# Hymba-style decoder step: weight sums and up-times-gate products of the FFN from GpSimd to VectorE, two scratch stores from SyncE's queue to ScalarE's

## Chip, cores and metric

The kernel runs on one core of one Trainium2 chip. The metric is device time in microseconds (us) for one execution. Three executions of the kernel before took 1408.3, 1409.23 and 1413.17 us; the median is 1409.23 us.

The engines are TensorE (PE in the rows, with its weight loads as PEld), VectorE (DVE), ScalarE (ACT), GpSimd (POOL) and SyncE (SP), which only starts transfers. Each takes its instructions in a fixed order: what stands behind an instruction that waits, waits too.

## What is computed

One step of a decoder trunk for 1024 prompt positions and 8 sample rows (1032 columns in all): a token mixer (gMLP and Mamba-2 heads side by side), cross-attention into 256 memory tokens, a SwiGLU FFN with hidden size 2816, and a final RMSNorm. The change touches the FFN alone:

```python
def swiglu(hn, w_gate, w_up, w_down):
    return (jax.nn.silu(hn @ w_gate) * (hn @ w_up)) @ w_down
```

## The kernel before

All activations lie with features on the 128 partitions and columns in the free dimension. Every fp32 matmul is made of three fp32r matmuls: each operand is split into a high part (a cast on ScalarE) and a low part (a subtraction on VectorE), by `split_from` (lines 276 to 278); `mm3` (line 158) issues high-high, high-low and low-high.

In the FFN, gate and up are computed by a Strassen-Winograd scheme with seven products P1 to P7 in place of eight. The weights come in pairs of panels: `items` lists, for each pair number `fp` from 1 to 10, a gate item and then an up item, each with both column halves (q = 0 of 256 columns, q = 1 of 264). After fp 6 stand two short items, gate and up of fp 0 for q = 1 only (its q = 0 half is done ahead of the stage by `first_pair`). `gate_up(n)` runs through the seven products of item n in the order P1, P6, P2, P7, P5, P4, P3. A product of a full item is 24 matmuls, 12 for each half.

Three accumulator banks (X, Y, Z) per half are shared by the products: P6 and P7 and P4 follow each other in Y, P5 and P3 in Z, P1 and P2 in X. Between two products in one bank, VectorE has to read it (lines 1296, 1303, 1305; `t` and `u`/`g` in the rows): P7 waits for line 1296, P4 for line 1303, P3 for line 1305, each for its own half. ScalarE copies P1 out (line 1294).

`prepare(step)` makes the weight operand `fw` of one product, up to five products ahead (`AHEAD`, line 1262). At P6 it also forms four sums of the raw panels `fr` (lines 1248 to 1251, tiles `ws`): on VectorE for the first two items, on GpSimd for the other 20. There is room for one raw pair, so the next pair's panels (line 1231, from SyncE's queue) are loaded when the last reader of the panel they replace is done.

When an up item has its P4 and P3, its results `u` are multiplied by the gate's `g` on GpSimd (lines 1315 and 1321). Then `down_operands` (line 1349) forms on VectorE the differences that the down projection needs (line 1359, `dx`), and stores `u` and `dx` into the scratch `x_d` (line 1366). `down_sums` (line 1386) forms sums `ds` of the down weights `dr` (line 1391, loaded by line 1384) and stores them into `s_d` (line 1397). The tiles `dr`, `ds` and `dx` share four buffers (tag `qu`): a `ds` has to wait until the `dx` that lay in its buffer has been stored. All these loads and stores are issued by SyncE, in one order.

Program order is not the order on the engines: the program is written once, and a scheduler orders each engine's instructions by its own estimate of times (`schedule_with_timeline_sim=True`), with the evacuations of the banks preferred (`tc.high_priority()`). A change of engine therefore moves neighbouring instructions too.

Of the kernel before, what the change touches and what calls it, by code (L numbers as in the profile page):

```python
# [43 lines left out]
def hymba_step(ctx: ExitStack, tc: tile.TileContext, I, O):  # L44
# [1105 lines left out]
    with ExitStack() as c3:  # L1150
# [86 lines left out]
        def prepare(step):  # L1237

            n, o = divmod(step, 7)
            if n >= len(items):  # L1240
                return
            load_pair(n)
            (a11, a12), (a21, a22) = ((t[:, 0:512], t[:, 512:D]) for t in wraw[n])
            nm = order_of(n)[o]
            if nm == "P6":
                eng = nc.vector if n < 2 else nc.gpsimd
                s1, s2, s3, s4 = wsum[n] = [n3.tile([P, 512], F32, tag="ws", bufs=4, name=f"ws{n}_{i}") for i in range(4)]
                eng.tensor_tensor(s1, a21, a22, op=ALU.add)  # L1248
                eng.tensor_tensor(s2, s1, a11, op=ALU.subtract)  # L1249
                eng.tensor_tensor(s4, a12, s2, op=ALU.subtract)  # L1250
                eng.tensor_tensor(s3, a11, a21, op=ALU.subtract)
            src = {"P1": a11, "P2": a12, "P4": a22}[nm] if nm in ("P1", "P2", "P4") else wsum[n][("P5", "P6", "P7", "P3").index(nm)]
            t = wp.tile([P, D], F32R, tag=("whi", "wlo")[step % 2], name=f"fw{step}")
            split_from(t[:, 0:512], t[:, 512:D], src)
            wop[step] = tuple(t[:, s].rearrange("p (k n) -> p k n", n=P) for s in (slice(0, 512), slice(512, D)))
            if o == 6:
                load_pair(n + 1)
# [8 lines left out]
        def gate_up(n, between):  # L1266
            x, fp, qs = items[n]
            bank = {q: {} for q in qs}
            tmp = {q: temps(q) for q in qs}
            res = {}  # L1270
            for q in qs:
                res[q] = piece(f"{x}{fp}_{q}")[:, :, : WQ[q]].rearrange("p (j h) n -> p j h n", j=2)
            for o, nm in enumerate(order_of(n)):
                for s in range(7 * n + o, 7 * n + o + AHEAD + 1):
                    if s not in wop:
                        prepare(s)
                if o == 4:
                    form_differences()
                between(o)
                hi, lo = wop[7 * n + o]  # L1280
                for q in qs:
                    w = WQ[q]
                    p1, u2, u3 = tmp[q]
                    b = "XXYYZZ"[("P1", "P2", "P6", "P7", "P5", "P3").index(nm)] if nm != "P4" else "Y"
                    if b not in bank[q]:
                        bank[q][b] = (gbank if (n % 2 if len(qs) == 1 else q) == 0 else mbank)(f"{x}{b}{fp}_{q}")
                    fresh = nm in ("P1", "P6", "P5")
                    ps = bank[q][b][:, :w]
                    xh, xl = XQ[q][nm]
                    mm3(ps, lambda k: (hi[:, k, :], lo[:, k, :]), lambda k: (xh[:, k, :], xl[:, k, :]), range(4), fresh=fresh, done=nm in ("P2", "P4", "P3"))  # L1290
                    r = res[q]
                    with tc.high_priority():
                        if nm == "P1":
                            nc.scalar.copy(p1, ps)
                        elif nm == "P6":
                            nc.vector.tensor_add(u2, p1, ps)
                        elif nm == "P2":
                            if x == "g":
                                nc.scalar.activation(r[:, 0, 0, :], ps, AF.Silu)
                            else:  # L1300
                                nc.vector.tensor_mul(r[:, 0, 0, :], gates[q][:, 0, 0, :], ps)
                        elif nm == "P7":
                            nc.vector.tensor_add(u3, p1, ps)  # L1303
                        elif nm == "P5":
                            nc.vector.tensor_add(r[:, 1, 1, :], u3, ps)
                        elif nm == "P4":
                            nc.vector.tensor_add(r[:, 1, 0, :], p1, ps)
                        else:
                            nc.vector.tensor_add(r[:, 0, 1, :], u2, ps)
                    if nm == "P4":  # L1310
                        t = r[:, 1, :, :]
                        if x == "g":
                            nc.scalar.activation(t, t, AF.Silu)
                        else:
                            nc.gpsimd.tensor_tensor(t, t, gates[q][:, 1, :, :], op=ALU.mult)  # L1315
                    elif nm == "P3":
                        t = r[:, 0, 1, :]
                        if x == "g":
                            nc.scalar.activation(t, t, AF.Silu)
                        else:  # L1320
                            nc.gpsimd.tensor_tensor(t, t, gates[q][:, 0, 1, :], op=ALU.mult)
            for q in qs:
                if x == "g":
                    gates[q] = res[q]
                else:
                    differences.append(lambda q=q, r=res[q]: down_operands(fp, q, r))
# [27 lines left out]
        def down_operands(fp, q, r):  # L1354

            w = WQ[q]
            r = r.rearrange("p j h n -> p (j h) n")
            t = piece(f"dx{fp}_{q}", "qu")[:, 0:3, :w]
            sub = lambda o, x, y: nc.vector.tensor_tensor(o, x, y, op=ALU.subtract)
            sub(t[:, 1], r[:, 3], r[:, 1])  # L1360
            sub(r[:, 1], r[:, 1], r[:, 0])
            sub(t[:, 0], r[:, 3], r[:, 1])
            sub(t[:, 2], r[:, 2], t[:, 0])
            for i, src in ((0, r), (4, t)):
                m = src.shape[1]
                nc.sync.dma_start(x_d[i : i + m, fp, :, 256 * q : 256 * q + w].rearrange("o p n -> p o n"), src)

        def form_differences():
            for work in differences:
# [16 lines left out]
        def down_sums(fp):  # L1386

            (a11, a12), (a21, a22) = ((t[:, 0], t[:, 1]) for t in dn[fp])
            t = [n3.tile([P, 2, 512], F32, tag="qu", bufs=4, name=f"ds{fp}_{i}") for i in range(2)]
            s1, s2, s3, s4 = t[0][:, 0], t[0][:, 1], t[1][:, 0], t[1][:, 1]  # L1390
            op = lambda o, x, y, k: nc.vector.tensor_tensor(o, x, y, op=k)  # L1391
            op(s1, a21, a22, ALU.add)
            op(s2, s1, a11, ALU.subtract)
            op(s3, a11, a21, ALU.subtract)
            op(s4, a12, s2, ALU.subtract)
            for i in range(2):
                nc.sync.dma_start(s_d[2 * i : 2 * i + 2, :, fp, :].rearrange("s p n -> p s n"), t[i])

        def prepare_down(n):

# [274 lines left out]
```

## Time and profile before

| | |
|---|---|
| median of three executions | 1409.23 us |
| the profiled execution | 1412.27 us, its span 1410.4 us |
| TensorE busy | 1369.1 us, 97% of the span |
| VectorE busy | 957.9 us, 68% |
| ScalarE busy | 626.1 us, 44% |
| GpSimd busy | 304.1 us, 22% |
| TensorE clock granted | 0.99 of full speed in the mean |
| transfers | 232.66 MB, 165 GB/s in the mean |

Busy shares are means over stages with different limits. In a timeline, the first number is the start in us from the span's start, the second the duration; what stands in square brackets is the time that the engine was idle just before, and what it waited for. TensorE's matmuls are pipelined, so a duration overlaps the next start; distances between starts are the safe measure.

### The profile page before, as it was taken

What the parts mean: (1) busy time and instruction counts of PE and PEld (TensorE: products, weight loads), DVE (VectorE), ACT (ScalarE), POOL (GpSimd) and SP (SyncE); (2) the same over time, 40 slices, a digit from 0 to 9 for tenths busy, and PEclk for the clock granted to TensorE, in tenths of its full rate; (3) what the DMA queues carried; (4) which work ended last, traced back from release to release, by engine and by line L of the source; (5) the groups of instructions that cost most, each with busy time, mean ns of one, the idle gap of its engine ahead of it and who ended that gap; (6) DMA issues with size and microseconds to landing.
All of it is one profiled execution on the core that took longest, in us unless ns stands there. A gap on an engine that the chain in (4) does not pass through costs nothing. (4 is left out here: it accounts for less than half of the span.)

```text
span 1410.4 us, 26083 instructions
## 1 busy us (share of the span) xinstructions
PE 1369.1 (97%) x10315; PEld 1305.8 (93%) x10315; DVE 957.9 (68%) x2021; ACT 626.1 (44%) x1131; POOL 304.1 (22%) x263
## 2 busy tenths in 40 slices
PE   8999999999999999999999999999899999999997
PEld 8889988899999978988999999999899999999997
DVE  7886689734533877778988666657766675656685
ACT  5666545234332645844563333223332343543654
POOL 3321122201221300000002333433444321003020
PEclk9999999999999999999999999999999999999999
DMA  8531344310642578378424545443645569656664
GB/s 302 192 98 48 96 125 115 92 54 30 236 154 76 167 268 324 94 270 299 129 83 158 161 159 160 143 141 108 206 149 181 161 210 325 204 169 183 205 190 133
DMA packets 145530, 232.66 MB, mean 165 GB/s; under 512 B 8328, under 2 KB 91880, under 8 KB 145024
## 3 DMA queue, kind: packets, MB, share of 16 engines
q1 hardware_dynamic: 145264, 230.94, 50.6%
q8 instruction: 81, 1.33, 0.4%
q14 instruction: 41, 0.34, 0.1%
q10 hardware_dynamic: 144, 0.05, 0.0%
HBM read 179.16 MB, written 51.81 MB: 164 GB/s over the span
## 5 line engine op out<-in xcount | busy, mean ns | idle before, releaser
L149 DVE TENSOR_TENSOR wl<-wr,wh 128x1024 fp32r<-128x1024 f32 x87 | 109.1, 1256 | 34.6 <-ACT wh L148 34.3
L148 ACT CAST wh<-wr 128x1024 fp32r<-128x1024 f32 (+1 forms) x89 | 92.2, 1038 | 85.3 <-PE g_gv L172 25.1
L277 ACT CAST fw<-ws 128x512 fp32r<-128x512 f32 x88 | 54.4, 622 | 125.9 <-POOL ws L1249 54.8
L278 DVE TENSOR_TENSOR fw<-ws,fw 128x512 fp32r<-128x512 f32 x88 | 81.1, 923 | 38.3 <-ACT fw L277 38.2
L1248 POOL TENSOR_TENSOR ws<-fr 128x512 f32<-128x512 f32 x20 | 26.8, 1339 | 236.9 <-DMA fr<-in_w_gate_dram 169.5
L277 ACT CAST fw<-fr 128x512 fp32r<-128x512 f32 x66 | 40.8, 619 | 80.3 <-PE m_uZ L172 20.1
L1578 PE MATMUL m_d<-xP,dwhi 128*128 128x264 f32 x448 | 64.1, 285 | 0.0
L278 DVE TENSOR_TENSOR xP<-xsP,xP 128x512 fp32r<-128x512 f32 (+2 forms) x84 | 54.9, 694 | 12.8 <-ACT xP L277 12.3
L278 DVE TENSOR_TENSOR dwlo<-dw,dwhi 128x1024 fp32r<-128x1024 f32 x32 | 39.8, 1245 | 34.7 <-ACT dwhi L277 34.6
L1578 PE MATMUL g_d<-xP,dwhi 128*128 128x256 f32 x448 | 63.0, 283 | 0.0
L278 DVE TENSOR_TENSOR fw<-fr,fw 128x512 fp32r<-128x512 f32 x66 | 55.9, 848 | 8.1 <-ACT fw L277 7.7
L1578 PEld LDWEIGHTS m_d<-xP,dwhi 128*128 128x128 f32 x448 | 58.5, 189 | 0.0
L1578 PEld LDWEIGHTS g_d<-xP,dwhi 128*128 128x128 f32 x448 | 57.7, 191 | 0.0
L277 ACT CAST xP<-xsP 128x512 fp32r<-128x512 f32 (+2 forms) x84 | 45.3, 588 | 23.9 <-DMA xsP<-x_d 15.0
L172 PE MATMUL m_uY<-sP,fw 128*128 128x264 f32 x396 | 53.7, 284 | 1.4 <-DVE fw L278 1.4
L277 ACT CAST dwhi<-dw 128x1024 fp32r<-128x1024 f32 x32 | 33.6, 1050 | 47.7 <-PE m_d L1578 37.2
L172 PE MATMUL g_gY<-sP,fw 128*128 128x256 f32 (+1 forms) x396 | 53.1, 283 | 0.0
L172 PE MATMUL m_gY<-sP,fw 128*128 128x264 f32 x360 | 49.5, 286 | 3.5 <-DVE t L1303 3.5
L172 PEld LDWEIGHTS m_uY<-sP,fw 128*128 128x128 f32 x396 | 50.1, 189 | 1.7 <-DVE fw L278 1.7
L172 PEld LDWEIGHTS m_gY<-sP,fw 128*128 128x128 f32 x360 | 45.6, 188 | 5.0 <-DVE t L1303 4.7
L172 PEld LDWEIGHTS g_gY<-sP,fw 128*128 128x128 f32 x396 | 49.7, 190 | 0.3
L172 PE MATMUL g_uY<-sP,fw 128*128 128x256 f32 x360 | 48.3, 283 | 1.7 <-DVE t L1303 1.0
(556 smaller groups left out, 3842.6 us busy)
## 6 DMA issues: line engine op xcount, KB each, us to landing
xsP<-x_d SPq DMA_DIRECT2D x35, 520.0 KB, 5.9
wr<-in_w_q_dram SPq DMA_DIRECT2D x24, 512.0 KB, 3.9
fr<-in_w_gate_dram SPq DMA_DIRECT2D x22, 512.0 KB, 3.6
fr<-in_w_up_dram SPq DMA_DIRECT2D x22, 512.0 KB, 3.7
dr<-in_w_down_dram SPq DMA_DIRECT2D x22, 512.0 KB, 5.4
s_d<-ds SPq DMA_DIRECT2D x22, 512.0 KB, 3.5
wr<-in_w_in_dram SPq DMA_DIRECT2D x20, 512.0 KB, 3.6
dw<-s_d SPq DMA_DIRECT2D x20, 512.0 KB, 4.5
```

Source lines behind the costliest of these rows:

```text
L148: nc.scalar.copy(hi[:, s], r[:, s])
L149: (nc.gpsimd if i == 0 else nc.vector).tensor_tensor(lo[:, s], r[:, s], f(hi[:, s]), op=ALU.subtract)
L172: ins = nc.tensor.matmul(ps, lhs(k)[a], rhs(k)[b], start=(fresh and i == 0), stop=(i == n - 1), skip_group_check=not (fresh and done))
L277: nc.scalar.copy(dst_hi, src)
L278: (eng or nc.vector).tensor_tensor(dst_lo, src, f(dst_hi), op=ALU.subtract)
L1248: eng.tensor_tensor(s1, a21, a22, op=ALU.add)
L1578: nc.tensor.matmul(ps[:, : WQ[q]], wdn[n](k)[a], x_at(nm, q, k)[b], start=(i == 0), stop=(i == 3 * NPAIR - 1))
```

## The change

Three edits in the FFN: the four weight sums of every item are made on VectorE; the products of up with gate are made on VectorE; the stores into `x_d` and `s_d` are issued from ScalarE's queue in place of SyncE's. No arithmetic changes.

```diff
@@ -1243,7 +1243,7 @@
             if nm == "P6":
-                eng = nc.vector if n < 2 else nc.gpsimd
+                eng = nc.vector
@@ -1312,13 +1312,13 @@
                         else:
-                            nc.gpsimd.tensor_tensor(t, t, gates[q][:, 1, :, :], op=ALU.mult)
+                            nc.vector.tensor_tensor(t, t, gates[q][:, 1, :, :], op=ALU.mult)
                     elif nm == "P3":
...
-                            nc.gpsimd.tensor_tensor(t, t, gates[q][:, 0, 1, :], op=ALU.mult)
+                            nc.vector.tensor_tensor(t, t, gates[q][:, 0, 1, :], op=ALU.mult)
@@ -1363,7 +1363,7 @@
-                nc.sync.dma_start(x_d[i : i + m, fp, :, 256 * q : 256 * q + w].rearrange("o p n -> p o n"), src)
+                nc.scalar.dma_start(x_d[i : i + m, fp, :, 256 * q : 256 * q + w].rearrange("o p n -> p o n"), src)
@@ -1394,7 +1394,7 @@
-                nc.sync.dma_start(s_d[2 * i : 2 * i + 2, :, fp, :].rearrange("s p n -> p s n"), t[i])
+                nc.scalar.dma_start(s_d[2 * i : 2 * i + 2, :, fp, :].rearrange("s p n -> p s n"), t[i])
```

The change moves 122 instructions from GpSimd to VectorE and 66 transfers from SyncE's queue to ScalarE's. What it does to the order is shown at two places, both in the gate item of fp 6, which stands behind the up item of fp 5 (`_0_` and `_1_` in a name are the halves; `g_` and `m_` in front are two groups of banks; the last numbers only tell tiles apart).

VectorE before, from the reading of P6 to that of P5:

```order
L1296 TENSOR_TENSOR t_10574<-t_10573,g_gY_0_10619 128x256
L1296 TENSOR_TENSOR t_10577<-t_10576,m_gY_1_10633 128x264
L278 TENSOR_TENSOR fw_10647<-fr_0_10615,fw_10647 128x512
L1391 TENSOR_TENSOR ds_0_10967<-dr_1_10832 128x512
L1303 TENSOR_TENSOR t_10575<-t_10573,g_gY_0_10619 128x256
L1391 TENSOR_TENSOR ds_0_10967<-ds_0_10967,dr_0_10831 128x512
L278 TENSOR_TENSOR fw_10684<-ws_1_10677,fw_10684 128x512
L1303 TENSOR_TENSOR t_10578<-t_10576,m_gY_1_10633 128x264
L278 TENSOR_TENSOR fw_10713<-fr_0_10615,fw_10713 128x512
L1391 TENSOR_TENSOR ds_1_10968<-dr_0_10831,dr_1_10832 128x512
L1391 TENSOR_TENSOR ds_1_10968<-dr_0_10831,ds_0_10967 128x512
L1305 TENSOR_TENSOR g_0_10579<-t_10575,g_gZ_0_10730 128x256
```

VectorE in the changed kernel, the part from the preparation behind P6 to the reading of P5:

```order
L278 TENSOR_TENSOR fw_10647<-fr_0_10615,fw_10647 128x512
L1248 TENSOR_TENSOR ws_0_10676<-fr_1_10616 128x512
L1249 TENSOR_TENSOR ws_1_10677<-ws_0_10676,fr_0_10615 128x512
L1303 TENSOR_TENSOR t_10575<-t_10573,g_gY_0_10619 128x256
L1250 TENSOR_TENSOR ws_3_10679<-fr_0_10615,ws_1_10677 128x512
L1251 TENSOR_TENSOR ws_2_10678<-fr_0_10615,fr_1_10616 128x512
L278 TENSOR_TENSOR fw_10684<-ws_1_10677,fw_10684 128x512
L1303 TENSOR_TENSOR t_10578<-t_10576,m_gY_1_10633 128x264
L1391 TENSOR_TENSOR ds_0_10967<-dr_1_10832 128x512
L278 TENSOR_TENSOR fw_10713<-fr_0_10615,fw_10713 128x512
L1391 TENSOR_TENSOR ds_1_10968<-dr_0_10831,dr_1_10832 128x512
L1305 TENSOR_TENSOR g_0_10579<-t_10575,g_gZ_0_10730 128x256
```

The four sums `ws` now stand around the first reading of P7 (line 1303), and the first `ds` has moved from ahead of both readings of P7 to behind them.

ScalarE in the changed kernel, the same gate item from its copy of P1 on:

```order
L1294 COPY t_10573<-g_gX_0_10584 128x256
L1366 DMA x_d<-u_0_10334 128x4x256
L1294 COPY t_10576<-m_gX_1_10598 128x264
L277 CAST fw_10612<-ws_3_10438 128x512
L1366 DMA x_d<-u_1_10335 128x4x264
L1366 DMA x_d<-dx_0_10716 128x3x256
L1366 DMA x_d<-dx_1_10723 128x3x264
L277 CAST fw_10647<-fr_0_10615 128x512
L1299 ACTIVATE g_0_10579<-g_gX_0_10584 128x256
```

The four stores of the up item before now stand between the copies of P1 and the casts of weights; on SyncE's queue they stood between the loads of `fr` and `dr`, which now follow each other there without a store.

## Rows read from the trace of the kernel before

**Rows 1.** The windows view, the stage of gate and up: us, busy by engine, clock, DMA

```profile
732.00:1176.00 444.00, 432.59 (x3552) 428.04 (x3551) 301.71 (x538) 143.99 (x275) 161.36 (x121) 1.00 0.52 164
```

**Rows 2.** The timeline of TensorE, starts that came late

```profile
831.35 1.73 PE L172 MATMUL m_gY<-sP,fw 128*128 128x264 f32 x12 [0.53 <-DVE t L1303]
...
914.79 1.73 PE L172 MATMUL m_gY<-sP,fw 128*128 128x264 f32 x12 [0.62 <-DVE t L1303]
...
956.54 1.71 PE L172 MATMUL m_gY<-sP,fw 128*128 128x264 f32 x12 [0.68 <-DVE t L1303]
...
997.91 0.75 PE L172 MATMUL m_uY<-sP,fw 128*128 128x264 f32 x4 [1.44 <-DVE fw L278]
1001.87 1.22 PE L172 MATMUL g_gX<-sP,fw 128*128 128x256 f32 x8 [2.11 <-ACT fw L277]
...
1079.19 1.70 PE L172 MATMUL g_uY<-sP,fw 128*128 128x256 f32 x12 [0.77 <-DVE t L1296]
1086.19 1.69 PE L172 MATMUL g_uY<-sP,fw 128*128 128x256 f32 x12 [0.96 <-DVE t L1303]
1108.53 1.74 PE L172 MATMUL m_gY<-sP,fw 128*128 128x264 f32 x12 [0.48 <-DVE t L1303]
```

**Rows 3.** The chain of waits, one pair of items apart: start, us, what

```profile
1125.12 1.43 PE g_uZ L172 x12
...
1165.47 1.43 PE g_uZ L172 x12
```

**Rows 4.** The timeline of VectorE, gate item of fp 6

```profile
951.99 0.76 DVE L1391 TENSOR_TENSOR ds<-dr 128x512 f32<-128x512 f32 x1 [4.81 <-DMA x_d<-dx]
...
953.00 1.45 DVE L1391 TENSOR_TENSOR ds<-ds,dr 128x512 f32<-128x512 f32 x1
954.37 1.78 DVE L278 TENSOR_TENSOR fw<-ws,fw 128x512 fp32r<-128x512 f32 x1
956.07 0.42 DVE L1303 TENSOR_TENSOR t<-t,m_gY 128x264 f32<-128x264 f32 x1
...
957.01 0.68 DVE L1391 TENSOR_TENSOR ds<-dr,dr 128x512 f32<-128x512 f32 x1
957.61 0.68 DVE L1391 TENSOR_TENSOR ds<-dr,ds 128x512 f32<-128x512 f32 x1
```

**Rows 5.** The timeline of GpSimd, the same item

```profile
949.53 1.29 POOL L1248 TENSOR_TENSOR ws<-fr 128x512 f32<-128x512 f32 x1 [7.08 <-DMA fr<-in_w_up_dram]
...
953.85 1.74 POOL L1251 TENSOR_TENSOR ws<-fr,fr 128x512 f32<-128x512 f32 x1
```

**Rows 6.** The lines view of VectorE by form: xcount, busy, mean ns, idle before

```profile
L278 DVE TENSOR_TENSOR fw<-ws,fw 128x512 fp32r<-128x512 f32 x88 | 81.1, 923 | 38.3 <-ACT fw L277 38.2
L278 DVE TENSOR_TENSOR fw<-fr,fw 128x512 fp32r<-128x512 f32 x66 | 55.9, 848 | 8.1 <-ACT fw L277 7.7 <-DMA s_d<-ds 0.3
...
L1359 DVE TENSOR_TENSOR u<-u 128x256 f32<-128x256 f32 x10 | 4.2, 417 | 0.0
```

**Rows 7.** The view of line 1248: xcount, duration ns min/median/max, starts

```profile
L1248 DVE TENSOR_TENSOR ws<-fr x2: 682/683/684, 727.4 to 745.6; 128x512 f32<-128x512 f32 x2
```

**Rows 8.** Views of lines 84 and 1366: issues (ns min/median/max), landing of the stores (us)

```profile
L84 ACTq DMA_DIRECT2D vecT<-in_vecs_dram x1: 397/397/397, 0.8 to 0.8; - x1
...
L1366 SPq DMA_DIRECT2D x_d<-u x22: 360/408/1818, 743.9 to 1179.3; - x22
...
DMA to landing us min/median/max: 3.1/7.4/10.3
```

**Rows 9.** The waits view, who waited for the loads of raw panels

```profile
POOL ws L1248 <- DMA fr<-in_w_gate_dram: 169.5, 10, 62.1
...
POOL ws L1248 <- DMA fr<-in_w_up_dram: 46.9, 7, 7.6
```

**Rows 10.** The timeline of VectorE and that of SyncE, near 1075 us

```profile
1074.98 0.69 DVE L1391 TENSOR_TENSOR ds<-dr 128x512 f32<-128x512 f32 x1 [4.34 <-issue]
...
1076.90 0.33 SPq L1231 DMA_DIRECT2D fr<-in_w_gate_dram  x1
```

## Prediction

> **What bounds the kernel now.** I read the windows view first, to see which engine has no time left in the stage that the change touches. TensorE was busy for 432.59 of the 444 us of gate and up [rows 1], VectorE for 301.71, ScalarE for 143.99, GpSimd for 161.36. The stage runs on TensorE's matmuls, at full granted clock (the 1.00 in the row), and no edit removes one. All that the change can win is the time in which TensorE stands: 444 - 432.59 = 11.41 us, plus what a stop costs behind it.
>
> Second, the timeline of TensorE, for where it stands. There is a pattern: in six gate items (the first at 831.35, the last at 1108.53) the second half's product P4 starts late, behind VectorE's reading of P7, line 1303 [rows 2]. What one such stop costs is read from distances. Without a stop, the same group of matmuls in two successive up items lies 1165.47 - 1125.12 = 40.35 us apart [rows 3]; with one, 956.54 - 914.79 = 41.75 us [rows 2]. So a stop costs 1.40 us, its idle time of 0.62 to 0.68 being only part of that, and the six cost 8.4 us. Outside the pattern stand 1.44 and 2.11 us around 1000 us, where the short items of fp 0 are, and 0.77 and 0.96 us near 1080 us [rows 2].
>
> Third, the timeline of VectorE in one of these gate items [rows 4]. VectorE stood for 4.81 us, until 951.99, because the first `ds` needs a buffer whose `dx` was still being stored. Then came what had piled up: a `ds` of 1.45 us, an `fw` of 1.78 us, and only at 956.07 the reading that TensorE needed. Undisturbed, the same `ds` takes 0.68 us, one starting 0.60 us behind the other (957.01, 957.61). GpSimd was making its sums at that time, the last from 953.85 for 1.74 us [rows 5]: VectorE's instructions with two SBUF inputs run slow beside it. The whole stage shows that too: the 88 `fw` from sums take 923 ns in the mean and the 66 from raw panels 848 [rows 6], while a VectorE sum without GpSimd beside it takes 683 [rows 7].
>
> **The change, part by part.** *Work for VectorE.* 20 items by four sums are 80 instructions of 0.683 us [rows 7]: 54.6 us. The products are 21 wide ones (two rows of up to 264), taken like a sum of 512: 21 x 0.70 = 14.7 us; and 21 narrow ones like a 256-wide subtraction of 0.417 us [rows 6]: 8.8 us. Together 78 us. Given back, with GpSimd silent: 88 x (0.923 - 0.69) + 66 x (0.848 - 0.69) = 20.5 + 10.4 = 31 us. VectorE's 301.71 us become about 349 of some 432, 81%: not the bound in the mean, so what counts is where the added instructions stand in its order.
>
> *The recurring stop.* In the new order of VectorE, both readings of P7 stand ahead of the first `ds`, so the wait for the store no longer delays them; the four sums stand around them instead. A walk in the old clock, with every step at 0.60 us (a reading at its duration of 0.42, rounded to 0.4): the up panel's second half had landed when GpSimd began at 949.53 [rows 5], and in the new queue of SyncE no store stands in front of it, so 949.53 is late. Two sums: 950.7. The first reading of P7: 951.1. Two sums and one `fw`: 952.9. The second reading: 953.3. TensorE wants its result at 956.54 - 0.68 = 955.86 [rows 2], so 2.6 us are in hand. Next are the `ds` and the reading of P5: the stores are issued no earlier than before, and the buffer was free at 951.99 [rows 4]; were the landing of 7.4 us as long as the longest of 10.3 [rows 8], it would be free at 954.9, the reading of P5 done by 955.9, and TensorE wants that one product half later, at about 957.3. So I take all six stops as gone: -8.4 us (bounds: 0, if a stop reappears in each, and -8.4).
>
> *The short items around 1000 us.* GpSimd's four sums take from 949.53 to 953.85 + 1.74 = 955.59, 6.1 us [rows 5]; on VectorE four steps of 0.60, 2.4 us. That would cover the 1.44 + 2.11 = 3.55 us there. But the two short items then hold 26 instructions of 0.60 (14 `fw`, 8 sums, 4 `ds`), 19 of 0.4 (11 readings, 8 differences) and two products for VectorE, about 24 us, against 14 halves of 1.44 us on TensorE (half of 40.35 / 14), 20.2 us. The lead of five products can carry that excess, or not. I take half: -1.8 us (bounds +3 and -3.55).
>
> *The stops near 1080 us.* A `ds` waited 4.34 us for the down panel, and behind it in VectorE's order stood the `fw` whose end lets SyncE issue the next gate panel, at 1076.90 only [rows 10]. In the new order this `fw` stands ahead of those four `ds`. Both waits go: -1.7 us (bounds 0 and -1.7).
>
> *The stores on ScalarE.* 44 into `x_d` and 22 into `s_d`: 66 issues of 0.40 us [rows 8], 26 us on an engine with 300 us to spare [rows 1]. Behind the first store of an item stands the copy of P1's second half, behind the others casts made up to five products ahead, five times 2.88 us (40.35 / 14). By the walk the data of all four are ready within 1 us of the old issue. I take 0; without that cover, 1.6 us for each of 11 up items. Transfers are the same bytes; SyncE's loads lose the stores in front of them, which I count as nothing, since the walk does not need it.
>
> Sum: 8.4 + 1.8 + 1.7 = 11.9, say 12 us. The profiled execution, 1412.27 us with a span of 1410.4, would become 1400.3 with a span of 1398.4. It lies 3.0 us above the median of 1409.23, so for the median I forecast **1397.2 us**.
>
> **The rivals.** *A: the waits for weights move onto VectorE (slower).* GpSimd stood 169.5 + 46.9 us waiting for the raw panels [rows 9], and that cost nothing, because nothing else was in its queue. Now the first sum waits in VectorE's order, with the readings of the banks behind it. The walk gives the point from which it decides: a panel that lands more than 2.6 us later than 949.53, past 952.1, stops TensorE, us for us. If each of ten pairs lost 3 us so (the spread of landings between 7.4 and 10.3 [rows 8]), that is +30, less 12: about 1427 us. For it: GpSimd began at the landing itself in 17 of 20 items. Against: without stores in front the loads should come sooner, not later. Chance 0.10.
>
> *B: ScalarE is held by the stores (slower or even).* An issue took up to 1.818 us on SyncE [rows 8]. One such in front of the copy of P1 in each of 11 items would give 11 x 1.8 = 20 us if nothing hid it, less 12: 1417 us. The copy has about two halves, 2.9 us, before TensorE needs its reader, so a single long issue is hidden, and it takes one together with a late `u` to show. Chance 0.05. The Trainium skill, Perfetto Trace Analysis, section "DMA Instruction — HWDGE (DVE, Sync)", says that the descriptor generator is shared by the issuing sequencers and locked for one at a time, and that the profiled time of an issue includes the wait for that lock; by it, two queues issuing at once would make the long issues commoner, and all 11 items at their worst would give those 1417 us. No run here shows two queues issuing at once: the one issue from ScalarE, 0.397 us, had none beside it that the row tells of.
>
> *C: the stop moves.* The `ds` behind the readings of P7 now stand ahead of that of P5; if the stores land later on the other queue, or if the short items cost 3 us more instead of 1.8 less, the gains shrink to nothing: -12 + 8.4 + 4.8 = +1.2, 1407 to 1411 us. Chance 0.13.
>
> *D: part of it.* Three of six stops stay, or the short items give nothing: -5 to -9, 1400 to 1404 us. Chance 0.22.
>
> **How the numbers follow.** The forecast of -12 us, with a spread down to all of 11.41 us and the knock-on of the six stops (6 x (1.40 - 0.68) = 4.3 us), so down to 1393.5, has 0.50. A change of 0.3%, 4.2 us, is about what a measurement of this kernel can tell from none. Faster by more than that: the forecast and D, 0.72. Within it: C, 0.13. Slower: A and B, 0.15. The range leaves those two out at the top and goes to C's upper end, 1411; below, it goes to the most that can be won, with 1.5 us for the scatter of runs: 1392.
>
> **What would show it.** In the profile of the changed kernel: TensorE's busy time unchanged and its idle time in gate and up down to 2 or 3 us; no wait of P4's second half on line 1303; the `fw` at 0.69 us throughout; VectorE near 349 us in the stage, GpSimd near 0 there; the issues on ScalarE at 0.4 us. Wrong would be shown by waits of `ws` on the raw panels with TensorE waiting for line 1296 or 1303 just behind them (A), by issues above 1 us on ScalarE (B), or by waits of P3 on line 1305 (C).

## The result, and the profile after

The changed kernel takes **1395.77 us** (median of four executions, 1392.78 to 1396.3) against 1408.76 us of the kernel before, timed beside it (1407.35 to 1413.17). The ratio is 0.9895, with a 95% interval of 0.9877 to 0.9913: 13 us faster. The forecast was 1397.2 us.

The profiled execution of the changed kernel took 1395.65 us, with a span of 1393.9 us. The first row is from its table of engines, the second from the windows view of gate and up, with the columns of [rows 1]:

```profile
PE 1365.7 (98%) x10315; PEld 1305.9 (94%) x10315; DVE 989.9 (71%) x2143; ACT 626.4 (45%) x1131; POOL 140.5 (10%) x141
```

```profile
732.00:1162.00 430.00, 428.11 (x3557) 427.27 (x3556) 333.30 (x664) 144.22 (x273) 0.00 (x0) 1.00 0.53 172
```

TensorE stands for 430 - 428.11 = 1.9 us of the stage, where it stood for 11.41 us [rows 1]. GpSimd does nothing there now. The timeline of TensorE has only two late starts of over 0.3 us in the whole stage, where the kernel before had twelve, eight of them in [rows 2]:

```profile
744.96 1.22 PE L172 MATMUL g_uX<-sP,fw 128*128 128x256 f32 x8 [0.99 <-ACT fw L277]
...
991.36 1.21 PE L172 MATMUL g_gX<-sP,fw 128*128 128x256 f32 x8 [0.81 <-ACT fw L277]
```

Neither is a wait for a reading of a bank, and the first stands in the kernel before as well (0.99 us at 746.96). The timeline of VectorE in the gate item of fp 6, the place of [rows 4], shows why:

```profile
940.77 0.69 DVE L278 TENSOR_TENSOR fw<-fr,fw 128x512 fp32r<-128x512 f32 x1 [0.56 <-ACT fw L277]
941.38 0.68 DVE L1248 TENSOR_TENSOR ws<-fr 128x512 f32<-128x512 f32 x1
942.10 0.69 DVE L1249 TENSOR_TENSOR ws<-ws,fr 128x512 f32<-128x512 f32 x1
944.08 0.42 DVE L1303 TENSOR_TENSOR t<-t,g_gY 128x256 f32<-128x256 f32 x1 [1.29 <-PE g_gY L172]
944.42 0.68 DVE L1250 TENSOR_TENSOR ws<-fr,ws 128x512 f32<-128x512 f32 x1
945.02 0.69 DVE L1251 TENSOR_TENSOR ws<-fr,fr 128x512 f32<-128x512 f32 x1
945.62 0.68 DVE L278 TENSOR_TENSOR fw<-ws,fw 128x512 fp32r<-128x512 f32 x1
946.23 0.42 DVE L1303 TENSOR_TENSOR t<-t,m_gY 128x264 f32<-128x264 f32 x1
946.56 0.68 DVE L1391 TENSOR_TENSOR ds<-dr 128x512 f32<-128x512 f32 x1
```

The `ds` follows the second reading of P7 and waits for nothing; no step takes more than 0.69 us. In the timeline of TensorE the second half of P4 starts here at 949.65, and the reading that it needs ran at 946.23. With the 0.68 us between wanting and starting, 949.65 - 0.68 - 946.23 = 2.7 us are in hand.

What the one execution won is read best from distances, since the start of the stage varies between profiled executions of kernels that are the same up to there (725.8 to 732.5 us among those below). From the first matmul group of the stage to the last one of its last up item (the `g_uZ` that starts at 1172.98 before and at 1156.27 now) it is 1172.98 - 732.50 = 440.5 us before and 1156.27 - 730.47 = 425.8 us now: **14.7 us**, of a difference of 16.5 in the spans. Another 2.0 us lie ahead of the stage, where the change does nothing. The same group of matmuls in successive up items, from the timeline of TensorE, shows where the 14.7 us come from. Before:

```profile
979.21 0.63 PE L172 MATMUL g_uZ<-sP3l,fw 128*128 128x256 f32 x4
1045.57 0.63 PE L172 MATMUL g_uZ<-sP3l,fw 128*128 128x256 f32 x4
1089.64 0.63 PE L172 MATMUL g_uZ<-sP3l,fw 128*128 128x256 f32 x4
1131.20 0.63 PE L172 MATMUL g_uZ<-sP3l,fw 128*128 128x256 f32 x4
```

Now:

```profile
971.75 0.63 PE L172 MATMUL g_uZ<-sP3l,fw 128*128 128x256 f32 x4
1033.80 0.63 PE L172 MATMUL g_uZ<-sP3l,fw 128*128 128x256 f32 x4
1074.15 0.63 PE L172 MATMUL g_uZ<-sP3l,fw 128*128 128x256 f32 x4
1114.49 0.63 PE L172 MATMUL g_uZ<-sP3l,fw 128*128 128x256 f32 x4
```

The distances are 66.36, 44.07 and 41.56 us before and 62.05, 40.35 and 40.34 us now: 4.3 us less with the short items of fp 0, 3.7 and 1.2 us less in the two pairs behind them. In the four pairs ahead, from 812.41 to 979.21 before (166.80 us) and from 810.36 to 971.75 now (161.39 us), it is 5.4 us. The rest sums to nothing: up to the first of these groups it is 1.2 us more, from there to the second 1.2 us less.

### The profile page after: what moved, and what is told of

Its sections match the earlier page's. It is cut to its first block, busy times and chain, and to the rows that moved or that the text cites. A ratio compares the mean times of both kernels' runs of the same rounds, so it can differ in the third digit from the quotient of the medians.

```text
span 1393.9 us, 25954 instructions
## 1 busy us (share of the span) xinstructions
PE 1365.7 (98%) x10315; PEld 1305.9 (94%) x10315; DVE 989.9 (71%) x2143; ACT 626.4 (45%) x1131; POOL 140.5 (10%) x141
## 4 chain that ended last, share of the span: by engine, by line
PE 85%; DVE 7%; DMA 6%; ACT 1%; issue 1%; DVEq 0%; SPq 0%; ACTq 0%
PE m_d L1578 8%; PE g_d L1578 8%; PE g_xbc L172 6%; PE g_wo L172 6%; PE m_uY L172 3%; PE g_xob L172 3%; PE g_gY L172 3%; PE g_gu L172 3%; PE m_gY L172 3%; PE g_uY L172 3%; PE g_z L172 3%; PE g_gX L172 2%; PE m_uZ L172 2%; PE m_uX L172 2%; PE m_gX L172 2%; PE g_gZ L172 2%
## 5 line engine op out<-in xcount | busy, mean ns | idle before, releaser
L278 DVE TENSOR_TENSOR fw<-ws,fw 128x512 fp32r<-128x512 f32 x88 | 60.4, 689 | 16.9 <-ACT fw L277 16.3
L278 DVE TENSOR_TENSOR fw<-fr,fw 128x512 fp32r<-128x512 f32 x66 | 45.4, 689 | 7.9 <-ACT fw L277 7.9
```

The lines of the kernel that those rows point to most:

```text
L278: (eng or nc.vector).tensor_tensor(dst_lo, src, f(dst_hi), op=ALU.subtract)
```

## The experiments

All medians and ratios are against the kernel before, timed in turn on the same chip. "Stage" is the distance just defined, of the profiled execution; "VectorE" and "GpSimd" are busy times of the windows view from 732 to 1162 us.

| kernel | median us | ratio, 95% interval | stage us | VectorE | GpSimd |
|---|---|---|---|---|---|
| before | 1408.76 to 1411.31 | | 440.5 | 292.4 | 158.4 |
| whole change | 1395.77 | 0.9895 [0.9877, 0.9913] | 425.8 | 333.3 | 0 |
| sums alone | 1399.91 | 0.9927 [0.9909, 0.9945] | 429.4 | 325.1 | 43.1 |
| products alone | 1395.85 | 0.9900 [0.9881, 0.9920] | 428.1 | 311.1 | 115.3 |
| stores alone | 1401.6 | 0.9937 [0.9922, 0.9952] | 432.3 | 303.7 | 157.3 |
| sums and products | 1395.24 | 0.9884 [0.9866, 0.9901] | 424.9 | 336.6 | 0 |
| products and stores | 1397.63 | 0.9905 [0.9880, 0.9930] | 430.3 | 301.7 | 113.3 |
| whole change + 4 idle sums | 1411.49 | 1.0012 [0.9996, 1.0029] | 440.1 | 370.3 | 112.9 |
| whole change + 2 idle sums | 1400.01 | 0.9929 [0.9903, 0.9954] | 430.7 | 352.8 | 53.5 |
| whole change + 4 idle copies | 1398.47 | 0.9915 [0.9887, 0.9942] | 426.9 | 346.4 | 65.0 |

The question was which of the edits brings the 13 us, and by which mechanism: the order of VectorE (a `ds` with a long wait standing ahead of the readings of P7), the slow VectorE instructions beside GpSimd, or the queue of the stores.

**Sums and products on VectorE, stores left on SyncE's queue.**

```diff
-                eng = nc.vector if n < 2 else nc.gpsimd
+                eng = nc.vector
...
-                            nc.gpsimd.tensor_tensor(t, t, gates[q][:, 1, :, :], op=ALU.mult)
+                            nc.vector.tensor_tensor(t, t, gates[q][:, 1, :, :], op=ALU.mult)
...
-                            nc.gpsimd.tensor_tensor(t, t, gates[q][:, 0, 1, :], op=ALU.mult)
+                            nc.vector.tensor_tensor(t, t, gates[q][:, 0, 1, :], op=ALU.mult)
```

> The kernel before with the first two edits alone: sums and products on VectorE, stores still on SyncE's queue. My sum gives it the whole gain: 1395 to 1400 us, no pattern, fw at 0.69 us. Rival (the stores pay): 1404 to 1410 us. Second rival (VectorE fills up, and it needs the loads to come earlier to pay): waits of line 1248 on the raw panels on VectorE with TensorE waiting behind, 1403 us or more.

It took 1395.24 us, in its stage 424.9 us, with one late start of TensorE over 0.3 us. The first two edits give all of the gain without the third.

**Sums alone.**

```diff
-                eng = nc.vector if n < 2 else nc.gpsimd
+                eng = nc.vector
```

> The first edit alone: the weight sums on VectorE, products still on GpSimd, stores on SyncE. If the sums beside VectorE's readings make the stops (GpSimd's last sum of 1.74 us lies on the slow fw), most of the gain is here: 1397 to 1402 us, and GpSimd busy in the stage falls from 161 to about 45 us. Rival (the products on GpSimd make u, dx and so the store late, which is what ds waits for): 1405 us or more.

It took 1399.91 us. The recurring stop is gone, and yet the `ds` stands ahead of both readings of P7 here. Its timeline of VectorE in the gate item of fp 6, to be laid beside [rows 4]:

```profile
943.37 0.69 DVE L1248 TENSOR_TENSOR ws<-fr 128x512 f32<-128x512 f32 x1 [1.82 <-DMA fr<-in_w_up_dram]
...
946.63 0.69 DVE L1391 TENSOR_TENSOR ds<-dr 128x512 f32<-128x512 f32 x1
947.24 0.42 DVE L1303 TENSOR_TENSOR t<-t,g_gY 128x256 f32<-128x256 f32 x1
947.57 0.42 DVE L1303 TENSOR_TENSOR t<-t,m_gY 128x264 f32<-128x264 f32 x1
```

The four sums stand ahead of the `ds`, and while VectorE makes them the store lands: from the issue of the last `dx` store (939.85, from the timeline of SyncE's queue) to the `ds` it is 6.8 us, where it was 6.6 before, but the `ds` waits for nothing, and behind it every step takes its undisturbed time. Over the stage the `ds` waits 2.2 us for stores, where it waited 33.1. The second half of P4 starts at 949.86, so 949.86 - 0.68 - 947.57 = 1.6 us are in hand. What is left is one wait of 2.20 us at the short items, for line 1303, and the stage is 4.5 us longer than with sums and products together.

**Stores alone.**

```diff
-                nc.sync.dma_start(x_d[i : i + m, fp, :, 256 * q : 256 * q + w].rearrange("o p n -> p o n"), src)
+                nc.scalar.dma_start(x_d[i : i + m, fp, :, 256 * q : 256 * q + w].rearrange("o p n -> p o n"), src)
...
-                nc.sync.dma_start(s_d[2 * i : 2 * i + 2, :, fp, :].rearrange("s p n -> p s n"), t[i])
+                nc.scalar.dma_start(s_d[2 * i : 2 * i + 2, :, fp, :].rearrange("s p n -> p s n"), t[i])
```

> The kernel before with the third edit alone: x_d and s_d stored from ScalarE's queue, sums and products still on GpSimd. My sum counts the stores as nothing: 1405 to 1412 us, the pattern of P4's second half waiting for line 1303 still there in five or six gate items, GpSimd's chain of sums still 5 to 6 us. Rival (the loads freed from the stores in SyncE's order are what pays): 1396 to 1401 us, the pattern gone with GpSimd unchanged. Second rival (issues hold ScalarE): above 1412 us with TensorE waiting for ScalarE's copies or casts.

It took 1401.6 us, and so the edit that the prediction had counted as nothing is worth 0.5 to 0.8% by itself. Its timeline of VectorE in the gate item of fp 6, to be laid beside [rows 4]:

```profile
945.52 0.69 DVE L1391 TENSOR_TENSOR ds<-dr 128x512 f32<-128x512 f32 x1 [3.16 <-DMA x_d<-dx]
946.12 0.42 DVE L1303 TENSOR_TENSOR t<-t,g_gY 128x256 f32<-128x256 f32 x1
946.45 1.46 DVE L1391 TENSOR_TENSOR ds<-ds,dr 128x512 f32<-128x512 f32 x1
947.84 1.78 DVE L278 TENSOR_TENSOR fw<-ws,fw 128x512 fp32r<-128x512 f32 x1
949.53 0.42 DVE L1303 TENSOR_TENSOR t<-t,m_gY 128x264 f32<-128x264 f32 x1
```

Everything of [rows 4] is still there: the order, the `ds` of 1.46, the `fw` of 1.78 us beside GpSimd. Only the wait in front is 3.16 us in place of 4.81, and that is enough for the second half of P4 to start without a wait (at 950.77 in the timeline of TensorE, 0.56 us later than the 0.68 behind the reading would allow). Over the stage the `ds` waited 19.4 us for stores, six times, where it waited 33.1 us, seven times, before. From the issue of the last `dx` store to the start of that `ds` it is 945.52 - 940.41 = 5.1 us here and 951.99 - 945.42 = 6.6 us before (issue from the timelines of ScalarE's and SyncE's queues). On SyncE's queue two loads of `dr` and one of `fr` stood right ahead of the `dx` stores, from 942.37 to 944.33 (here one of these `dr` loads goes out at 928.39 already); that they delay the landing fits, but was not tried by itself.

The Trainium skill, DMA: Bandwidth & Descriptors, section "Issuing engines are not separate DMA queues", says that transfers run on the same 16 DMA engines whichever engine starts them, and that several issuers save only the time of issuing. The trace does not bear out the "only": bytes and transfers are the same, and the other queue alone gave a ratio of 0.9937. In the item read, the last `dx` store was issued at most 0.12 us behind the end of its `dx` in either kernel (945.30 and 945.42 before, 940.37 and 940.41 here), so what came sooner is not its issue but its landing.

**Products alone.**

```diff
-                            nc.gpsimd.tensor_tensor(t, t, gates[q][:, 1, :, :], op=ALU.mult)
+                            nc.vector.tensor_tensor(t, t, gates[q][:, 1, :, :], op=ALU.mult)
...
-                            nc.gpsimd.tensor_tensor(t, t, gates[q][:, 0, 1, :], op=ALU.mult)
+                            nc.vector.tensor_tensor(t, t, gates[q][:, 0, 1, :], op=ALU.mult)
```

> The second edit alone: the products of up with gate on VectorE, weight sums still on GpSimd, stores on SyncE. My theory: 1405 to 1410 us, since the wait for the store is at most 1 us shorter and the sums still slow the ds and the fw ahead of line 1303. Rival (the chain u, dx, store, ds decides): 1398 to 1402 us, the wait of ds for x_d gone or under 2 us.

A miss: with 1395.85 us its median is that of the whole change (its stage of 428.1 us is 2.3 us longer, all of it at the short items, 64.39 us against 62.05), though GpSimd makes its 80 sums as before, and `fw` is as slow beside them as before (873 and 824 ns in the mean by the lines view, against 923 and 848 [rows 6]). Its timeline of VectorE in the gate item of fp 6:

```profile
941.58 0.42 DVE L1303 TENSOR_TENSOR t<-t,g_gY 128x256 f32<-128x256 f32 x1 [2.25 <-PE g_gY L172]
...
943.56 0.42 DVE L1303 TENSOR_TENSOR t<-t,m_gY 128x264 f32<-128x264 f32 x1
943.90 0.68 DVE L1391 TENSOR_TENSOR ds<-dr 128x512 f32<-128x512 f32 x1
```

Two things have changed. The scheduler now puts the `ds` behind both readings of P7, as it does where the sums are moved. And the `ds` no longer waits there: over the whole stage 0.7 us, once. A product takes 0.69 us on VectorE where it took 1.29 on GpSimd, with a hand-over there and one back; counted from the start of the up item's last group of P3 (`m_uZ`, at 939.36 before and 930.81 here), the first `dx` store is issued 5.0 us later before (944.38) and 4.2 us later here (935.01). Which of the two counts for more was not separated: the order is the scheduler's, and the two came together.

So each edit removes the recurring stop in a way of its own. The products take the wait of the `ds` away and move it behind the readings; the sums leave it ahead of them, but fill the time of its wait with work; the stores leave it there and shorten its wait. Common to the three is that the readings of P7 no longer stand behind a long wait of the `ds`.

**Products and stores.**

```diff
-                eng = nc.vector
+                eng = nc.vector if n < 2 else nc.gpsimd
```

(against the whole change)

> Second and third edit together: products on VectorE, stores from ScalarE's queue, the weight sums still on GpSimd. Theory (each edit shortens the same wait of the first ds, and once it is gone there is nothing more to win): 1394 to 1398 us, as products alone, no wait of ds for x_d over 2 us, fw still at 0.82 to 0.97 us in the mean. Rival (the gains of the two edits add up, 0.0063 and 0.0100 of the time): 1388 to 1391 us.

It took 1397.63 us: nothing adds up. The recurring stop can be removed once, and what the two leave is above all at the short items (late starts of 2.78 us at 990.42, for line 1296, and of 1.44 us at 1015.13, for line 1305).

**The whole change and the one without stores, again.** The same two kernels as above, in more rounds side by side.

> The changed kernel a second time, beside the one without the third edit on the same chip. Theory (with sums and products on VectorE the stores' queue decides nothing): the two agree within 0.15%, 1394 to 1397 us both. Rival (the stores help here too, or hold ScalarE): a difference of over 0.3%, 4 us or more.

> First and second edit, the stores on SyncE, a second time, beside the whole change on the same chip. Theory: within 0.15% of the whole change, 1394 to 1397 us. Rival: a difference of over 0.3%, 4 us or more, either way.

They took 1396.01 us (ratio 0.9901 [0.9879, 0.9924]) and 1394.73 us (0.9883 [0.9861, 0.9905]). The intervals overlap by most of their length. On top of the other two edits the third shows no gain, and if anything else then a loss of some 0.1%.

**Four idle sums on GpSimd.** Is it needed that GpSimd is silent? The changed kernel, with sums that nobody reads; the order on VectorE, ScalarE and TensorE stays that of the changed kernel. In this kernel and the next two, line numbers are up to 4 higher (the sums are lines 1249 to 1252, the reading of P7 is line 1307).

```diff
+        idle_out = n3.tile([P, 448], F32, tag="idle", bufs=1, name="idle_out")
...
                 eng.tensor_tensor(s3, a11, a21, op=ALU.subtract)
+                if n >= 2:
+                    for _ in range(4):
+                        nc.gpsimd.tensor_tensor(idle_out, s1[:, 0:448], s2[:, 0:448], op=ALU.add)
```

> The changed kernel with four idle sums more on GpSimd in each of the 20 items from n = 2 on (ws + ws into a tile that nobody reads, 128 x 448); the order of VectorE, ScalarE and TensorE is that of the changed kernel. Theory (the long wait of the first ds for its buffer made the recurring stop; slow VectorE instructions beside GpSimd alone do not): fw and ds beside the idle sums take 1.2 to 1.8 us again, the mean of fw rises from 0.69 to between 0.75 and 0.95 us, and TensorE's idle time in gate and up stays under 5 us: 1395 to 1399 us. Rival (the slow instructions beside GpSimd are enough): P4's second half waits for line 1303 again in several gate items, 1402 to 1410 us.

The time lies outside both ranges. The median is 1411.49 us (1404.94 to 1415.96 in ten executions, of which the profiled one is the fastest), and the stage is 440.1 us long: the whole gain is gone. TensorE stands for 430 - 418.1 = 11.9 us of the window from 732 to 1162 us, where my theory had under 5.

But the recurring stop did not come back, and there the theory held. P4's second half waits for the reading of P7 in no gate item, and the four pairs that gave 5.4 us above are 40.34 to 40.37 us long, as in the changed kernel; the one ahead of them has 39.31 us in place of 37.67. In the gate item of fp 6 the reserve is just used up. The timelines of VectorE and of TensorE:

```profile
945.87 0.41 DVE L1307 TENSOR_TENSOR t<-t,m_gY 128x264 f32<-128x264 f32 x1
```

```profile
946.63 1.60 PE L172 MATMUL m_gY<-sP,fw 128*128 128x264 f32 x12
```

946.63 - 0.68 - 945.87 = 0.1 us are in hand, where it was 2.7: from 941.40 on, two sums and an `fw` stand ahead of this reading, and they take 4.5 us where the changed kernel takes 1.8 (944.42 to 946.23). The loss lies at the short items and behind them:

```profile
968.72 0.63 PE L172 MATMUL g_uZ<-sP3l,fw 128*128 128x256 f32 x4
...
1040.06 0.63 PE L172 MATMUL g_uZ<-sP3l,fw 128*128 128x256 f32 x4
```

That is 71.34 us, where the changed kernel has 62.05 (971.75 to 1033.80): 9.3 of the 14.3 us lost. Another 2.8 and 0.6 us are lost in the two pairs behind. The timeline of VectorE in the up item of fp 7, which lies in this stretch:

```profile
1029.04 0.69 DVE L1249 TENSOR_TENSOR ws<-fr 128x512 f32<-128x512 f32 x1 [1.99 <-DMA fr<-in_w_gate_dram]
...
1031.53 1.59 DVE L1251 TENSOR_TENSOR ws<-fr,ws 128x512 f32<-128x512 f32 x1
1033.04 1.64 DVE L1252 TENSOR_TENSOR ws<-fr,fr 128x512 f32<-128x512 f32 x1
1034.61 1.62 DVE L278 TENSOR_TENSOR fw<-ws,fw 128x512 fp32r<-128x512 f32 x1
1036.15 0.41 DVE L1307 TENSOR_TENSOR t<-t,g_uY 128x256 f32<-128x256 f32 x1
```

The timeline of GpSimd in this item, and that of TensorE:

```profile
1031.41 5.81 POOL L1255 TENSOR_TENSOR idle_out<-ws,ws 128x448 f32<-128x448 f32 x4 [10.36 <-DVE ws L1250]
```

```profile
1036.61 1.69 PE L172 MATMUL g_uY<-sP,fw 128*128 128x256 f32 x12 [2.46 <-DVE t L1307]
```

Three instructions of VectorE that start 0.60 us apart when it has SBUF to itself start 1.5 us apart (1031.53, 1033.04, 1034.61, 1036.15). That is 3 x 0.94 = 2.8 us. At this place too the changed kernel has 2.7 us in hand: its reading runs at 1027.04, and TensorE starts at 1030.45, without a wait. So the slowing alone would about be covered; the wait for a panel comes on top, 1.99 us where the changed kernel has 0.24, and TensorE stands. This is rival A of the prediction in small: sums wait for panels in VectorE's order, with the readings behind them.

**Two idle sums.**

```diff
-                    for _ in range(4):
+                    for _ in range(2):
```

> The changed kernel with two idle sums on GpSimd per item in place of four, VectorE's order unchanged. Theory (what counts is how much later VectorE gets through an item that it has to itself otherwise; some 2 us per item are in hand before TensorE stops, and four idle sums cost VectorE about 1.9 us per item): VectorE busy in the stage some 20 us over the changed kernel's instead of some 39, hardly a stop of TensorE, 1395 to 1400 us. Rival (each microsecond of slowing is handed on to TensorE): half of the 15 us, 1401 to 1405 us.

1400.01 us, at the edge of what the theory expected: with half of the idle sums VectorE is 19.5 us busier and the stage 4.9 us longer; with all of them it is 37 us busier and the stage 14.3 us longer. The loss grows faster than the load, which fits a reserve that covers a part of it. It too lies at the short items and in the pair behind them (3.8 and 1.2 us, by the same distances); everywhere else the distances are those of the changed kernel. The two slowed sums of each item, from the lines view of VectorE (mean of 22, two of which have no idle sum beside them):

```profile
L1251 DVE TENSOR_TENSOR ws<-fr,ws 128x512 f32<-128x512 f32 x22 | 30.9, 1406 | 0.0
L1252 DVE TENSOR_TENSOR ws<-fr,fr 128x512 f32<-128x512 f32 x22 | 26.5, 1203 | 0.0
```

Against 0.69 us alone that is (1.41 - 0.69) + (1.20 - 0.69) = 1.2 us per item, less than the 2.7 in hand.

Part of this loss is TensorE's clock. Behind the longest stop of this kernel, 2.29 us ahead of 991.55, the granted clock is 0.50 from 994 to 996 us, the lower of its two levels (1.2 in place of 2.4 GHz). The windows view has it in the column behind GpSimd's:

```profile
994.00:996.00 2.00, 2.00 (x11) 2.00 (x11) 0.00 (x0) 0.00 (x0) 0.00 (x0) 0.50 0.94 368
```

The 20 matmuls from 992.60 to 996.56 take 3.96 us here; in the changed kernel the same ones take 2.44 us (992.41 to 994.85). So 1.5 of the 4.9 us are clock. The four-sum kernel, sums alone and stores alone have one such stretch each, also behind a stop at the short items. It does not follow every stop: behind the 2.78 us of products and stores, and behind the 1.44 and 2.11 us of the kernel before, the granted clock stays at 1.00.

**Four idle copies.** Is it the load on GpSimd as such, or the hold that its instructions have on the tiles `ws`?

```diff
-                        nc.gpsimd.tensor_tensor(idle_out, s1[:, 0:448], s2[:, 0:448], op=ALU.add)
+                        nc.gpsimd.tensor_copy(idle_out, s1[:, 0:448])
```

> The changed kernel with four idle copies on GpSimd per item (one input each, ws into the idle tile, 128 x 448) in place of four idle sums. Control for the load on GpSimd itself and for the hold that it has on the tiles ws. Theory (it is the sharing of SBUF accesses that slows VectorE, and copies share less of them): ws and fw beside the copies take under 1.0 us, 1395 to 1400 us. Rival (any GpSimd instruction beside VectorE, or the hold on the tiles, does it): ws at 1.4 us and more, 1408 to 1413 us, as with four sums.

1398.47 us, stage 426.9 us. As many instructions hold the tile `s1`, and only 1.1 us of the stage are lost; the lines view of VectorE has the same two sums at

```profile
L1252 DVE TENSOR_TENSOR ws<-fr,fr 128x512 f32<-128x512 f32 x22 | 21.1, 959 | 0.0
...
L1251 DVE TENSOR_TENSOR ws<-fr,ws 128x512 f32<-128x512 f32 x22 | 18.2, 826 | 0.0
```

So it is not the number of instructions, which is that of the four sums. Nor is it GpSimd's time alone: 65.0 us of copies make VectorE 346.4 - 333.3 = 13.1 us busier, while 53.5 us of sums (two of them per item) make it 19.5 us busier. What differs is that a sum reads two inputs and a copy one. The hold is answered in part: the copies hold `s1` alone, the idle sums `s2` too; but the view of the tile `idle_out` names nobody who waited for the idle sums.

The Trainium skill, SBUF — State Buffer, section "Who interferes with whom", says that a VectorE instruction with two SBUF inputs contends with a GpSimd instruction that reads SBUF, while one with at most one SBUF input, outside the two-port modes, does not. The trace agrees: in the four-sum kernel the sums and `fw` take 1.6 us, and the readings of banks, with one input in SBUF, keep 0.41 us.

## Why the prediction was right, and where it was not

**The total** was right: 12 us forecast, 13.0 measured. The sum was made for the stage, and there the profiled execution won 14.7, 2.8 us more than the 11.9 of the sum; nearly all of this stands at the short items. That the median came out closer than the stage is luck.

**The recurring stop.** The mechanism was right: a `ds` that waits for a store stands ahead of the readings of P7, and behind the wait comes a pile. In the new order it stands behind them, no P4 waits for line 1303, and the 2.6 us that the walk gave for the reserve were measured as 2.7. Its size: the four pairs up to fp 6 won 5.4 us and the last of the six places 1.2, 1.3 us each where 1.40 was forecast. What failed is what I took to be needed. The walk moved the sums, took the silence of GpSimd with them, and relied on the new order, all as one thing. The runs took them apart. Products alone, with GpSimd's sums beside VectorE, are enough. Sums alone are enough with the `ds` ahead of both readings, so the order is not needed. And with four idle sums on GpSimd the stop stays away, so the silence is not needed for it either, though it leaves 0.1 us of the reserve. The silence counts at the short items and in the pairs behind them, where four idle sums lost 9.3 + 2.8 + 0.6 = 12.7 us. In the changed kernel no `ds` waits for a store at all, so what its new place is worth there no run shows.

**"SyncE's loads lose the stores in front of them, which I count as nothing".** This step failed. Alone the edit gives a ratio of 0.9937, by shortening the wait of the `ds` from 4.81 to 3.16 us in the item read. Within the whole change the 0 was right, by the two kernels run side by side; but a term that is 0 because another edit removed the same wait first is another statement than the one that I made.

**The products** had only a cost in the sum, 23.5 us of VectorE's time. That they shorten the way from `u` over `dx` and its store to the `ds`, and that the order changes with them, was left out; alone they gave as much as everything by the median, and 12.4 of the 14.7 us by the stage.

**The short items** were under-sized: I took half of the 3.55 us, 1.8, and 4.3 were won; of the waits only 0.81 us was left. The distance also holds a late start of 0.60 us at 1033.24, which I had not listed. My 24 us of VectorE's work against 20.2 us of TensorE's did not bind, but VectorE has least to spare here (51.5 us busy of the 62 from 972 to 1034), and it is here that the idle sums cost most.

**Near 1080 us** the forecast was 1.7 us and one recurring stop of 1.40; this pair won 3.7. I read the 4.34 us as a wait for the down panel; the row names no releaser ("issue"). It fits the panel: from the issue of the second half (1066.91, from the timeline of SyncE's queue) to that `ds` it is 8.07 us, and the longest landing in the view of line 1384 is 8.1.

**VectorE's load.** I forecast 349 us, 47 more than before. From the first group of the stage to 5 us behind the start of its last one (732.50 to 1178.00 before, 730.47 to 1161.30 now) it went from 303.2 to 334.1 us, 31 more. The added work was right: sums at 0.69 us, products at 0.70 and 0.43. Two things were not. I left out of the relief the 44 `ds`, which by the lines view took 37.9 us before and 30.4 now, and 1 us of differences `dx`. And I added durations to a busy time of the windows view, which counts once the time in which two instructions overlap: at 0.69 us each and 0.60 us from start to start they add up to more than the engine is busy. By durations VectorE's instructions in these two stretches went from 332.2 to 372.8 us, 41 more. The rows of the view of lines 1248 and 1315 and of `fw`, after:

```profile
L1248 DVE TENSOR_TENSOR ws<-fr x22: 683/688/694, 725.3 to 1124.2; 128x512 f32<-128x512 f32 x22
```

```profile
L1315 DVE TENSOR_TENSOR u<-u,g x21: 691/702/711, 771.4 to 1156.0; 128x528 f32<-128x528 f32 x11, 128x512 f32<-128x512 f32 x10
```

```profile
L278 DVE TENSOR_TENSOR fw<-ws,fw 128x512 fp32r<-128x512 f32 x88 | 60.4, 689 | 16.9 <-ACT fw L277 16.3
...
L278 DVE TENSOR_TENSOR fw<-fr,fw 128x512 fp32r<-128x512 f32 x66 | 45.4, 689 | 7.9 <-ACT fw L277 7.9
```

**The rivals.** A began and did not reach TensorE: VectorE waited for gate panels, by the waits view,

```profile
DVE ws L1248 <- DMA fr<-in_w_gate_dram: 5.9, 7, 1.5
```

at most 1.5 us at a time, less than the reserve of 2.6. By another way one did reach it: the late start of 0.81 us at 991.36 stands behind a cast of ScalarE that had waited 0.80 us for a gate panel. It takes the slower VectorE of the idle sums to make A decide. B did not come, though its sign did: the issues of the `dx` stores on ScalarE were not at 0.40 us but above 1, as the view of line 1366 shows.

```profile
L1366 ACTq DMA_DIRECT2D x_d<-u x22: 366/366/1149, 741.9 to 1161.5; - x22
L1366 ACTq DMA_DIRECT2D x_d<-dx x22: 366/1048/1372, 748.3 to 1163.5; - x22
...
DMA to landing us min/median/max: 3.2/6.4/7.9
```

The timeline has no wait of TensorE or of VectorE behind them. Nor do such issues need two queues at once: with the products alone, where SyncE issues every transfer of the stage, the median issue of a `dx` store is 1.14 us. C and D did not come: no wait for line 1305 is in the timeline of TensorE, and none of the six stops stayed.

## What to carry to other kernels

Several edits that remove the same wait do not add up: price each by what it does alone and by what is left of the wait once the others are made. When an instruction that waits for a transfer stands in an in-order engine ahead of work that the bounding engine wants, it can be moved behind that work, other work can be put in front of it to fill its wait, or its wait can be made shorter, by data that come sooner or from another queue; here each of the three edits alone was enough for this stop, so try them alone before all together. Before work goes from GpSimd to VectorE, count the reserve of VectorE's readers in us per item, at the place where VectorE has most to do, and make sure that what stays on GpSimd does not eat it. Here a reserve of 2.7 us just covered the slowing by four idle sums in the gate item read; at the short items and behind them it did not, and most of the gain was lost there.

## What the runs showed that was not expected

Some store issues are long, on either queue. With the products on VectorE both `dx` stores are ready together, and on SyncE's queue (products alone) the timeline has

```profile
935.01 2.41 SPq L1366 DMA_DIRECT2D x_d<-dx  x2
```

2.41 us for two, where before each took 0.42 and 0.53 us (944.38 and 945.42), with a third store issued between them (0.47 us at 944.90). On ScalarE's queue in the changed kernel the same pair takes 2.44 us, while the issues into `s_d` take 366 or 367 ns throughout. Standing close together is not enough to make them long, then: the three before follow each other within 0.1 us. What the issue waits for no row tells.

The median over executions and the stage of one profiled execution do not rank the kernels alike: products alone has 1395.85 us and 428.1 us, the whole change 1395.77 and 425.8. The stage of products alone began at 728.0 us, that of the whole change at 730.5, and up to there both are the same program. A difference of 2 us between kernels should be read from distances within the stage, or not at all.
